# Seven-product pairs in six output projection chunks, row sums of y, rows on three partition groups, and one plan for all attention groups

## The chip, the cores and the metric

The kernel runs on one core of a Trainium2 chip. The metric is the device time of one execution in microseconds (us), taken as the median of the runs. TensorE (PE) multiplies, VectorE (DVE) and ScalarE (ACT) work on the elements, and SyncE (SP) issues most of the DMAs. Everything is in float32; matrix products are made from operands split into a high and a low half (fp32r), three products in place of one.

## The reference

One encoder layer on x of 256 tokens by 4096. The stream is first normalised with an embedding norm; then, cut to what matters:

```python
def hybrid_layer(x, w_in, conv_w, sink, w_out, ln_g, ln_b):
    p = x @ w_in                       # 4096 to 26 chunks of 512
    ...
    y_conv = c_b * centred_short_conv(c_c * c_h, conv_w) * jax.nn.silu(c_z)
    y_attn = banded_window_attention(a_q, a_k, a_v, sink) * jax.nn.silu(a_z)
    y = jnp.concatenate([y_conv, y_attn], axis=-1) @ w_out      # 4096 x 4096
    return layer_norm(DN_ALPHA * x + y, ln_g, ln_b)
```

Two big products, by w_in and by w_out, hold nearly all the work. Between them stand a gated short convolution and a windowed attention with 16 heads in four groups; behind the second stand a residual and a norm.

## The kernel before

**Tiles and steps.** x, normalised and transposed, lies in xT as 32 k-tiles (128 of the 4096 rows of w each), each as high and low halves. The weights stream by in steps. A step of kind "s" is one DMA of 1024 KB (four k-tiles by 512 columns), and 24 matmuls of 512 columns: four k-tiles, two token tiles, three products of halves. A step of kind "S", a pair, is one DMA of 512 KB holding two k-tiles as half blocks, on which VectorE makes four more blocks by sums (lines 133 to 135); seven products of sums then stand in for eight (Strassen's scheme, the two k-tiles and two token tiles by two column halves), 21 matmuls of 256 columns. The scheme needs sums of x's blocks as well (x_sums, line 556, kept in SC) and adds its partial results, collected in the PSUM tile pacc, to the chunk's end (pair_copy on ScalarE, pair_sums on VectorE, lines 592 to 595).

**Stages.** The 26 input chunks come first: K and V with eight "s" steps each, the other 24 in the order "sSsSSsSsSSs", six pairs. While a chunk streams, the attention or convolution work of the chunks before is done between its steps, at step numbers kept in a table (`at`). For an attention group the table is SPREAD, for the last of the four DENSE, which puts the same heads' operations closer together. Then comes the output: seven chunks of 512 columns and two of 256, all "s", 64 steps. y lies where x lay, in xT, in the order Y_ORDER.

**One step of the output loop.** For step j: the matmuls of j (mm_out, lines 809 to 811); functions due at j; SP issues the load of the next step for which a raw weight buffer is free; ScalarE makes the high half of step j + 3 (split_hi, line 149), VectorE its low half (split_lo, line 153). The high and low halves have three buffers each, so the high half of step j + 3 waits for the end of step j. The raw pieces have three buffers (w0, w1, w2) in the output stage, and one or two more in the input stage; a load waits for the low half that was made from its buffer's last piece.

**End of a chunk.** Behind the loop of chunk n, end_out and end_out2 run for both token tiles: residual plus accumulator (line 816), statistics (817), and the product with the norm's gain (821). Then res_load(n + 1) issues five DMAs of 256 KB on SP for the next chunk: three rows broadcast to all partitions (gb) and two pieces of x (xc). residual(n) makes the normalised x from them with three operations a tile (lines 791 to 794), at step 2 of chunk n (step 7 for chunk 0).

**Rows and the tail.** The norm's gain and bias are needed as five rows of halves, which build_rows writes at chunk 1's step 4: a load of 32 × 128 into lnw, a cast and a difference (lines 768 and 769), and small DMAs into `rows` (line 771). The tail (finish_lhs, finish_tr, finish_out) makes a 5-row operand from the statistics, transposes it, and adds its product with rows to R. All four spare PSUM tiles serve it under the name att. The last step's halves are made one step early, into a raw buffer.

What sets the order on each engine is the order of these calls; nothing is rescheduled.

## Time and profile before

| what | us |
|---|---|
| median of 3 runs | 1552.48 (1551.56 to 1552.85) |
| the profiled execution's own time | 1551.65 |
| its span | 1549.9 |
| mean granted clock of TensorE | 0.996 |

A span runs from the first to the last recorded instruction. In the views, a row of the timeline gives start, duration, engine, line, operation, and in brackets the idle time ahead of it with the engine that ended it; a row of waits gives the total, the number and the longest; a group gives busy time, mean in ns, and the idle time before. Of the span, the attention of the last group lies near 500 to 550, the output stage runs from about 1179 on, and the tail from about 1515.

### The profile page before, as it was taken

The page shows a single profiled execution, that of the slowest core. Times are in us where ns is not written, and L with a number is a line of the kernel's source. Part 1 is how long each engine was busy: PE and PEld are TensorE (multiplying, and loading weights), DVE is VectorE, ACT ScalarE, POOL GpSimd, SP SyncE. Part 2 cuts the span into 40 slices and gives each one's busy share as a digit, 9 for nine tenths or more (in the row PEclk, how much of TensorE's full clock was granted, in tenths as well). Part 3 has the DMA queues.
Part 4 walks back from the last instruction along what each step waited for, and adds up shares of the span by engine and source line. Part 5 has one row for each costly group of instructions (what it writes and reads, how often), then busy time and mean ns, then how long its engine had stood idle before and what let it go on. Part 6 is the DMA issues. An engine that isn't in the chain of part 4 may idle for free.

```text
span 1549.9 us, 20599 instructions
## 1 busy us (share of the span) xinstructions
PE 1528.0 (99%) x8478; PEld 1320.0 (85%) x8478; DVE 1223.9 (79%) x1358; ACT 738.6 (48%) x620; POOL 1.3 (0%) x7
## 2 busy tenths in 40 slices
PE   7999999999999999999999999999999999999997
PEld 4888888888888888888888888888888888888896
DVE  8678798888898878898888888888987665566656
ACT  4544546556565555545454445444555333333331
POOL 0000000000000000000000000000000000000000
PEclk9999999999999999999999999999999999999998
DMA  7545554555545456556556565566556565666662
GB/s 300 211 140 194 202 193 177 188 176 184 197 165 189 152 196 239 201 197 224 191 180 214 195 214 199 189 200 214 193 202 260 207 245 220 226 224 226 222 222 109
DMA packets 64078, 312.95 MB, mean 202 GB/s; under 512 B 7696, under 2 KB 11248, under 8 KB 38384
## 3 DMA queue, kind: packets, MB, share of 16 engines
q1 hardware_dynamic: 63408, 310.06, 56.6%
q8 instruction: 66, 1.08, 0.3%
q10 hardware_dynamic: 576, 1.57, 0.3%
q14 instruction: 28, 0.23, 0.0%
HBM read 303.66 MB, written 7.86 MB: 201 GB/s over the span
## 4 chain that ended last, share of the span: by engine, by line
PE 89%; DVE 5%; ACT 2%; issue 2%; DMA 1%; SPq 0%; DVEq 0%; ACTq 0%
PE acc L189 15%; PE acc L191 15%; PE acc L190 14%; PE acc L809 7%; PE acc L811 7%; PE acc L810 7%; PE pacc L214 4%; PE pacc L213 4%; PE pacc L215 4%; PE acc L214 3%; PE acc L213 3%; PE acc L215 3%; DVE wlo L153 2%; ACT whi L149 1%; PE att L420 1%
## 5 line engine op out<-in xcount | busy, mean ns | idle before, releaser
L149 ACT ACTIVATE whi<-w 128x2048 fp32r<-128x2048 f32 (+1 forms) x341 | 623.0, 1827 | 738.0 <-PE acc L191 301.6
L153 DVE TENSOR_TENSOR wlo<-w,whi 128x2048 fp32r<-128x2048 f32 (+1 forms) x341 | 739.6, 2175 | 259.8 <-ACT whi L149 257.9
L189 PE MATMUL acc<-whi,xT 128*128 128x512 f32 x1072 | 424.4, 396 | 0.0
L191 PE MATMUL acc<-whi,xT 128*128 128x512 f32 x1072 | 420.2, 392 | 0.0
L190 PE MATMUL acc<-wlo,xT 128*128 128x512 f32 x1072 | 417.3, 389 | 0.7 <-DVE wlo L153 0.7
L191 PEld LDWEIGHTS acc<-whi,xT 128*128 128x128 f32 x1072 | 201.3, 188 | 46.9
L190 PEld LDWEIGHTS acc<-wlo,xT 128*128 128x128 f32 x1072 | 201.4, 188 | 41.7 <-DVE wlo L153 1.0
L189 PEld LDWEIGHTS acc<-whi,xT 128*128 128x128 f32 x1072 | 201.5, 188 | 37.4
L809 PE MATMUL acc<-whi,xT 128*128 128x512 f32 (+1 forms) x560 | 208.1, 372 | 0.0
L811 PE MATMUL acc<-whi,xT 128*128 128x512 f32 (+1 forms) x560 | 206.9, 369 | 0.0
L810 PE MATMUL acc<-wlo,xT 128*128 128x512 f32 (+1 forms) x560 | 205.3, 367 | 0.4 <-DVE wlo L153 0.4
L810 PEld LDWEIGHTS acc<-wlo,xT 128*128 128x128 f32 x560 | 105.1, 188 | 19.6 <-DVE wlo L153 0.8
L811 PEld LDWEIGHTS acc<-whi,xT 128*128 128x128 f32 x560 | 105.1, 188 | 19.6
L809 PEld LDWEIGHTS acc<-whi,xT 128*128 128x128 f32 x560 | 105.3, 188 | 17.1 <-issue 0.4
L133 DVE TENSOR_TENSOR w<-w 128x512 f32<-128x512 f32 x144 | 98.2, 682 | 0.0
L213 PE MATMUL pacc<-whi,xT 128*128 128x256 f32 x288 | 82.4, 286 | 0.0
L214 PE MATMUL pacc<-wlo,SC 128*128 128x256 f32 x288 | 81.0, 281 | 0.0
L215 PE MATMUL pacc<-whi,SC 128*128 128x256 f32 x288 | 80.8, 280 | 0.0
L213 PE MATMUL pacc<-whi,SC 128*128 128x256 f32 x288 | 80.7, 280 | 0.0
L214 PE MATMUL acc<-wlo,xT 128*128 128x256 f32 x288 | 80.5, 279 | 0.0
L214 PE MATMUL pacc<-wlo,xT 128*128 128x256 f32 x288 | 80.5, 279 | 0.0
L213 PE MATMUL acc<-whi,xT 128*128 128x256 f32 x288 | 80.4, 279 | 0.0
(192 smaller groups left out, 1634.8 us busy)
## 6 DMA issues: line engine op xcount, KB each, us to landing
w<-in_wi SPq DMA_DIRECT2D x134, 1024.0 KB, 4.9
w<-in_ws SPq DMA_DIRECT2D x144, 512.0 KB, 3.3
w<-in_wo SPq DMA_DIRECT2D x64, 1024.0 KB, 4.9
yl<-yd SPq DMA_DIRECT2D x7, 512.0 KB, 6.9
xc<-in_x SPq DMA_DIRECT2D x14, 256.0 KB, 6.5
x<-in_x SPq DMA_DIRECT2D x6, 512.0 KB, 7.3
first<-in_wi SPq DMA_DIRECT2D x2, 1024.0 KB, 8.1
...
```

Source lines behind the costliest of these rows:

```text
L133: nc.vector.tensor_tensor(r[:, 4:6, :], r[:, 1:3, :], r[:, 0:1, :].to_broadcast([P, 2, HW]), op=ALU.add)
L149: nc.scalar.activation(part(j, wh[j]), part(j, raw[j]), AF.Copy)
L153: nc.vector.tensor_tensor(part(j, wl[j]), part(j, raw.pop(j)), part(j, wh[j]).bitcast(F32), op=ALU.subtract)
L189: nc.tensor.matmul(a, xh, hk, start=(first and k == 0), stop=False)
L190: nc.tensor.matmul(a, xh, lk, start=False, stop=False)
L191: nc.tensor.matmul(a, xl, hk, start=False, stop=(last and k == PK - 1))
L213: nc.tensor.matmul(o, ah, hi[:, w, :], start=(opens and p == 0), stop=False)
L214: nc.tensor.matmul(o, ah, lo[:, w, :], start=False, stop=False)
L215: nc.tensor.matmul(o, al, hi[:, w, :], start=False, stop=(closes and last))
L809: nc.tensor.matmul(o, yh, hk, start=(s == 0), stop=False)
L810: nc.tensor.matmul(o, yh, lk, start=False, stop=False)
L811: nc.tensor.matmul(o, yl, hk, start=False, stop=(s == KT - 1))
```

## The change

- In the output, chunks 1 to 6 get four pairs each in place of eight k-tiles: chunk 1 in the order "ssSsSsSsSs", chunks 2 to 6 "sSsSssSsSs". Chunk 0 (eight "s") and the two narrow chunks stay. There are 76 steps instead of 64. A chunk's pairs are gathered by pair_copy and pair_sums as in the input, and plus_res adds the residual to them at the chunk's last step; end_out adds the accumulator.
- The sums of y's blocks are made by x_sums at chunk 0's step 6 and chunk 1's steps 0, 1 and 2 into a new SC of four blocks; scratch is a part of R.
- The high half of step j + 3 is now issued ahead of the functions due at j, and sums(j + 4) ahead of the low half.
- residual takes two operations a tile instead of three, at step 5 of chunk 1 and step 4 of chunks 2 to 6 instead of 2.
- The rows lie on three partition groups (0, 32, 64), so that rows takes 1536 columns instead of 4096; the tail fills three groups of t5. Loading (rows_load, chunk 2 step 4) and splitting (rows_split, chunk 2 step 8) are apart, and 15 small DMAs fill the rows instead of six.
- The tail's PSUM tiles alternate between two pools, and the last chunk's residual tile takes SC's place and is loaded at chunk 7's step 0 instead of chunk 6's step 4. The last step's halves are made in their turn.
- The last attention group uses SPREAD; DENSE goes. open_pc comes three steps later.

```diff
+OUT = 100
+OP = 4
+OUT_ORDERS = ["s" * 8, "ssSsSsSsSs"] + ["sSsSssSsSs"] * 5 + ["", ""]
...
-        bs = [(wpool, f"w{k}") for k in range(N_W)] + (extra if steps[j][0] != "out" else [])
+        bs = [(wpool, f"w{k}") for k in range(N_W)] + (extra if j < N_IN else [])
...
-                (sc(0), 5, p1[:, 1, :], True, False), (x(a, 1), 6, p0[:, 1, :], False, True),
+                (sc(0), 5, p1[:, 1, :], True, False), (x(a, 1) if ci < OUT else sc(3), 6, p0[:, 1, :], False, True),
...
-    DENSE = [(2, q_tr, 0), (3, q_lo, 0), (7, q_tr, 1), (8, q_lo, 1)] + head(0, 4, 5, 6, 7, 8, 9, 10, 12, 13) + head(
-        1, 5, 6, 7, 8, 9, 12, 13, 14, 15) + head(2, 9, 10, 11, 12, 13, 14, 15, 17, 18) + head(
-        3, 11, 12, 13, 14, 15, 16, 17, 19, 20)
...
+        if SC.shape[3] == 4:
+            return halves(SC[:, p, 0, :, :], SC[:, p, 1, :, :], s)
...
-            for t, f, a in SPREAD if g < NG - 1 else DENSE:
+            for t, f, a in SPREAD:
...
-                at(j + 1, open_pc)
+                at(j + 4, open_pc)
...
+    RB = [(0, 0), (0, 1), (0, 2), (32, 0), (32, 1), (32, 2), (64, 0), (64, 1)]
...
-    def build_rows():
-        for src, slots_h, slot_l in ((ln_g, (0, 1), 2), (ln_b, (3,), 4)):
-            w = p2.tile([KT, P], F32, name="lnw")
+    lnw = {}
+
+    def rows_load():
+        for k, src in enumerate((ln_g, ln_b)):
+            w = lnw[k] = R[0:KT, k, D - 4 * P:D - 3 * P]
             nc.sync.dma_start(out=w, in_=src.rearrange("(a b) -> a b", b=P))
-            hl = p2.tile([KT, 2, P], F32R, name="lnhl")
+
+    def rows_split():
+        for k, (slots_h, slot_l) in enumerate((((0, 1), 2), ((3,), 4))):
+            w, hl = lnw[k], R[0:KT, k, D - 3 * P:D - P].bitcast(F32R).rearrange("p (a b) -> p a b", a=2)
             nc.vector.tensor_copy(hl[:, 0, :], w)
             nc.vector.tensor_tensor(hl[:, 1, :], w, hl[:, 0, :].bitcast(F32), op=ALU.subtract)
-            for r in slots_h:
-                nc.sync.dma_start(out=rows[r:r + 1, :].bitcast(F32), in_=hl[:, 0, :].bitcast(F32))
-            nc.sync.dma_start(out=rows[slot_l:slot_l + 1, :].bitcast(F32), in_=hl[:, 1, :].bitcast(F32))
+            for b, a0, n in ((0, 0, 12), (32, 12, 12), (64, 24, 8)):
+                for r, h in [(r, 0) for r in slots_h] + [(slot_l, 1)]:
+                    nc.sync.dma_start(out=rows[b + r:b + r + 1, 0:n * P].bitcast(F32), in_=hl[a0:a0 + n, h, :].bitcast(F32))
...
+            z = p2.tile([P, OP * 2 * 4, HT], F32, name="z", tag="SC").rearrange("p a b -> p (a b)")
...
-            nc.vector.tensor_scalar(xc[:, i, :], xc[:, i, :], musd[:, i, 0:1], musd[:, i, 2:3],
-                                    op0=ALU.subtract, op1=ALU.mult)
-            nc.vector.tensor_tensor(xc[:, i, :], xc[:, i, :], gb[:, 0, :], op=ALU.mult)
-            nc.vector.tensor_tensor(xc[:, i, :], xc[:, i, :], gb[:, 1, :], op=ALU.add)
-
-    oacc = {}
+            nc.vector.scalar_tensor_tensor(xc[:, i, :], xc[:, i, :], musd[:, i, 0:1], gb[:, 0, :],
+                                           op0=ALU.subtract, op1=ALU.mult)
+            nc.vector.scalar_tensor_tensor(xc[:, i, :], xc[:, i, :], musd[:, i, 2:3], gb[:, 1, :],
+                                           op0=ALU.mult, op1=ALU.add)
...
+    def plus_res(n):
+
+        c0, w, _, _ = chunks[n]
+        e = st_.pop(("e", OUT + n))
+        for i in range(2):
+            nc.vector.scalar_tensor_tensor(e[:, i, :], res[n][1][:, i, :], ALPHA, e[:, i, :], op0=ALU.mult, op1=ALU.add)
...
-        nc.vector.scalar_tensor_tensor(r, res[n][1][:, i, :], ALPHA, oacc.pop((n, i)), op0=ALU.mult, op1=ALU.add)
+        a = acc.pop((OUT + n, i))
+        if npairs(OUT + n):
+            nc.vector.tensor_tensor(r, a, r, op=ALU.add)
+        else:
+            nc.vector.scalar_tensor_tensor(r, res[n][1][:, i, :], ALPHA, a, op0=ALU.mult, op1=ALU.add)
...
-        nc.vector.tensor_copy(t5[:, i, 0:3:2], ch.bitcast(F32).to_broadcast([P, 2]))
+        for b in (0, 32, 64):
+            if b:
+                nc.vector.tensor_copy(t5[:, i, b + 1:b + 2], t5[:, i, 1:2])
+            nc.vector.tensor_copy(t5[:, i, b:b + 3:2], ch.bitcast(F32).to_broadcast([P, 2]))
...
-            sh = ps_att.tile([P, 512], F32, name="att")
-            nc.tensor.matmul(sh, lhs5[0:5, i, :], rows[0:5, sl], start=True, stop=True)
+            sh = (ps_att if c % 2 else ps_p).tile([P, 512], F32, name="att" if c % 2 else "pacc")
+            b, k = RB[c]
+            nc.tensor.matmul(sh, lhs5[b:b + 5, i, :], rows[b:b + 5, k * W:(k + 1) * W], start=True, stop=True)
...
+    for k in range(OP):
+        at(N_IN + (6, 8, 9, 10)[k], lambda k: x_sums(k, R[:, 1, D - 4 * S:D]), k)
     for n, (c0, w, pk, j0) in enumerate(chunks):
-        npc = KT // pk
-        for q in range(npc):
-            j = j0 + q
-            mm_out(j, n, (0,) if n == ncs - 1 else (0, 1))
+        us = out_units(n)
+        np_ = sum(u[0] == "opair" for u in us)
+        for t, (kind, _, q) in enumerate(us):
+            j = j0 + t
+            if kind == "opair":
+                mm_pair(j)
+            else:
+                mm_out(j, n, (0,) if n == ncs - 1 else (0, 1))
+            if j + 3 < len(steps):
+                split_hi(j + 3)
             for fn, a in later.pop(j, []):
                 fn(*a)
+            if kind == "opair" and q == np_ - 1:
+                pair_copy(OUT + n)
+                at(j + 1, pair_sums, OUT + n)
+                at(j + 1, plus_res, n)
             if j == N_IN + 5:
                 open_p2()
                 res_load(0)
             loads(j)
-            if j + 3 < len(steps) - 1:
-                split(j + 3)
-            if j + 4 == len(steps) - 1:
-                split(j + 4)
-            if q == (0 if n == ncs - 1 else 7 if n == 0 else min(2, npc - 1)):
+            sums(j + 4)
+            if j + 3 < len(steps):
+                split_lo(j + 3)
+            if t == (0 if n == ncs - 1 else 2 if not np_ and n else (7, 5, 4)[min(n, 2)]):
                 residual(n)
-            if n == 1 and q == 4:
-                build_rows()
+            if n == 2 and t == 4:
+                rows_load()
+            if n == 2 and t == 8:
+                rows_split()
                 nc.scalar.activation(small.tile([P, 1], F32, name="sd", bufs=1), eps_t, AF.Sqrt)
-            if n == ncs - 3 and q == 4:
+            if n == ncs - 2 and t == 0:
                 res_load(ncs - 1)
```

VectorE at the opening of chunk 1. wlo is a low half; R, xc and gb are the output, the residual's x and its rows. Before, from the second end_out of chunk 0 on:

```order
L816 SCALAR_TENSOR_TENSOR R_10252<-xc_10262,acc_10038 128x512
L817 BN_STATS s21_10254<-R_10252 128x6
L821 TENSOR_TENSOR R_10252<-R_10252,gb_10261 128x512
L153 TENSOR_TENSOR wlo_10383<-w0_10268,whi_10381 128x2048
L153 TENSOR_TENSOR wlo_10413<-w1_10298,whi_10411 128x2048
L153 TENSOR_TENSOR wlo_10443<-w2_10328,whi_10441 128x2048
```

Now, from the same place on:

```order
L859 SCALAR_TENSOR_TENSOR R_10249<-xc_10262,acc_10038 128x512
L860 BN_STATS s21_10251<-R_10249 128x6
L864 TENSOR_TENSOR R_10249<-R_10249,gb_10261 128x512
L578 TENSOR_TENSOR R_10249<-xT_86 128x512
L583 TENSOR_TENSOR R_10249<-R_10249 128x128 x4
L446 TENSOR_TENSOR SC_10253<-R_10249,SC_10253 128x512
L154 TENSOR_TENSOR w2_10305<-w2_10305 128x512
L155 TENSOR_TENSOR w2_10305<-w2_10305 128x256
L156 TENSOR_TENSOR w2_10305<-w2_10305 128x256
L174 TENSOR_TENSOR wlo_10399<-w1_10268,whi_10385 128x2048
L578 TENSOR_TENSOR R_10249<-xT_86 128x512
```

The low half of step 3 (wlo_10399, before wlo_10383) stood directly behind end_out; now the x_sums of two k-tiles and the sums of step 4 stand between.

VectorE at the turn from chunk 2 to chunk 3. Before:

```order
L816 SCALAR_TENSOR_TENSOR R_10252<-xc_10625,acc_10635 128x512
L817 BN_STATS s21_10254<-R_10252 128x6
L821 TENSOR_TENSOR R_10252<-R_10252,gb_10624 128x512
L153 TENSOR_TENSOR wlo_10922<-w1_10813,whi_10920 128x2048
L153 TENSOR_TENSOR wlo_10952<-w2_10843,whi_10950 128x2048
L153 TENSOR_TENSOR wlo_10982<-w0_10873,whi_10980 128x2048
```

Now (w0_11090 is the half piece of step 6 of chunk 3, w2_11042 the piece of step 5):

```order
L857 TENSOR_TENSOR R_10249<-acc_10715,R_10249 128x512
L860 BN_STATS s21_10251<-R_10249 128x6
L864 TENSOR_TENSOR R_10249<-R_10249,gb_10704 128x512
L174 TENSOR_TENSOR wlo_11092<-w0_10954,whi_11088 128x1792
L174 TENSOR_TENSOR wlo_11121<-w1_10985,whi_11117 128x2048
L154 TENSOR_TENSOR w0_11090<-w0_11090 128x512
L155 TENSOR_TENSOR w0_11090<-w0_11090 128x256
L156 TENSOR_TENSOR w0_11090<-w0_11090 128x256
L174 TENSOR_TENSOR wlo_11154<-w2_11042,whi_11147 128x2048
```

The sums of step 6 stand ahead of the low half of step 5.

SP at the same turn, before:

```order
L116 DMA w0_10873<-in_wo 128x2048
L781 DMA gb_10885<-in_emb_g_row 128x512
L782 DMA gb_10885<-in_emb_b_row 128x512
L783 DMA gb_10885<-in_ln_g 128x512
L785 DMA xc_10886<-in_x 128x512 x2
L116 DMA w1_10918<-in_wo 128x2048
```

Now:

```order
L137 DMA w2_11042<-in_wo 128x2048
L813 DMA gb_11055<-in_emb_g_row 128x512
L814 DMA gb_11055<-in_emb_b_row 128x512
L815 DMA gb_11055<-in_ln_g 128x512
L817 DMA xc_11056<-in_x 128x512 x2
L135 DMA w0_11090<-in_ws 128x1024
L137 DMA w1_11119<-in_wo 128x2048
```

The five loads of the residual stood ahead of a full piece; now they stand ahead of the half piece on which the sums of step 6 wait.

More of the change, by code (lines that the diff above doesn't have):

```diff
@@ L60, in units, with out_units, npairs @@
     return us
+def out_units(n):
+    if CHUNKS[n] < W:
+        return [("out", OUT + n, q) for q in range(KT * CHUNKS[n] // PIECE)]
+    q, p, us = 2 * npairs(OUT + n) // PK, 0, []
+    for u in OUT_ORDERS[n]:
+        if u == "s":
+            us.append(("out", OUT + n, q))
+            q += 1
+        else:
+            us.append(("opair", OUT + n, p))
+            p += 1
+    assert q == NPC
+    return us
+def npairs(ci):
+    return PAIRS[ci] if ci < OUT else OUT_ORDERS[ci - OUT].count("S")
 IN_STEPS = [u for ci in range(len(IN_ORDER)) for u in units(ci)]
 IN_PIECES = [u[1:] for u in IN_STEPS if u[0] == "in"]
-IN_PAIRS = [u[1:] for u in IN_STEPS if u[0] == "pair"]
 N_IN = len(IN_STEPS)
+OUT_STEPS = [u for n in range(len(CHUNKS)) for u in out_units(n)]
+ALL_PAIRS = [u[1:] for u in IN_STEPS + OUT_STEPS if u[0] in ("pair", "opair")]
+OUT_PIECES = [u[1:] for u in OUT_STEPS if u[0] == "out"]
 @with_exitstack
@@ L83, in encoder_kernel @@
     ctx.enter_context(tc.manual_schedule())
-    steps = list(IN_STEPS)
+    steps = IN_STEPS + OUT_STEPS
     chunks = []
-    c0 = 0
-    for w in CHUNKS:
-        pk = PIECE // w
-        chunks.append((c0, w, pk, len(steps)))
-        for q in range(KT // pk):
-            steps.append(("out", c0 * KT // PIECE, q))
-        c0 += w
+    for n, w in enumerate(CHUNKS):
+        chunks.append((sum(CHUNKS[:n]), w, PIECE // w, steps.index(out_units(n)[0])))
+    is_pair = lambda j: steps[j][0] in ("pair", "opair")
     raw, wh, wl = {}, {}, {}
@@ L112, in load @@
             to = raw[j] = pool.tile([P, PIECE], F32, name=name, bufs=1)
[L113 to L114 removed]
+        if is_pair(j):
+            nc.sync.dma_start(out=to[:, 0:4 * HW], in_=ws[ALL_PAIRS.index((a, b))])
         else:
[L116 removed]
+            nc.sync.dma_start(out=to, in_=wi[IN_PIECES.index((a, b))] if kind == "in" else wo[OUT_PIECES.index((a, b))])
     def loads(j):
@@ L128, in sums @@
     def sums(j):
-        if j >= len(steps) or steps[j][0] != "pair":
+        if j >= len(steps) or not is_pair(j):
             return
@@ L137, in part @@
     def part(j, t):
-        return t[:, HW:] if steps[j][0] == "pair" else t
+        return t[:, HW:] if is_pair(j) else t
     def half_tile(j, name):
@@ L199, in mm_pair @@
         hi, lo = (t.pop(j).rearrange("p (b w) -> p b w", w=HW) for t in (wh, wl))
-        last = p == PAIRS[ci] - 1
+        last = p == npairs(ci) - 1
         if p == 0:
@@ L747, in open_p2 @@
     def open_p2():
-        nonlocal p2, R, st2, ms2, rows, t5, lhs5, ps_att
+        nonlocal p2, R, st2, ms2, rows, t5, lhs5, SC
         ph.close()
         phs.close()
-        pps.close()
-        ps_att = ctx.enter_context(tc.tile_pool(name="ps_att3", bufs=4, space=PSUM))
         p2 = ctx.enter_context(tc.tile_pool(name="p2", bufs=1))
@@ L892, in encoder_kernel @@
     finish_out(1, range(8))
+    pps.close()
 ctx_rows = {}
```

49 lines of the change are left out of this document (29 added, 20 removed).

## The prediction

> **What bounds the kernel now.** I read the busy shares first, then what TensorE waited for, then busy time by stretch.
>
> ```profile
> PE 1528.0 (99%) x8478; PEld 1320.0 (85%) x8478; DVE 1223.9 (79%) x1358; ACT 738.6 (48%) x620; POOL 1.3 (0%) x7
> ...
> PE att L836 <- DVE t L831: 3.2, 1, 3.2
> PE att L516 <- DVE s L482: 1.5, 1, 1.5
> PE att L516 <- ACT p L509: 0.5, 1, 0.5
> PE acc L810 <- DVE wlo L153: 0.4, 1, 0.4
> ```
>
> TensorE is busy 99% of the span, so time is won only with fewer matmul cycles or in the few waits listed. The rest is told by stretches (columns: start:end, stretch, then busy time and count of PE, PEld, DVE, ACT, POOL, the granted clock, DMA share, GB/s):
>
> ```profile
> 515.00:545.00 30.00, 27.87 (x166) 24.27 (x165) 28.52 (x41) 16.67 (x25) 0.00 (x0) 1.00 0.37 123
> 599.50:642.00 42.50, 42.50 (x251) 37.52 (x250) 37.38 (x44) 23.14 (x19) 0.00 (x0) 1.00 0.62 221
> 1240.00:1270.00 30.00, 29.59 (x130) 23.97 (x129) 15.81 (x16) 12.98 (x8) 0.00 (x0) 1.00 0.56 209
> 1284.00:1328.00 44.00, 44.00 (x194) 36.09 (x193) 25.81 (x20) 15.31 (x8) 0.00 (x0) 1.00 0.63 221
> 1537.00:1543.00 6.00, 3.26 (x7) 1.90 (x7) 4.10 (x15) 0.56 (x2) 0.00 (x0) 0.61 0.13 48
> ```
>
> An input chunk with six pairs (second row) keeps VectorE busy 37.4 of 42.5 us, an output chunk without pairs (fourth row) 25.8 of 44. The change takes matmul cycles out of the output and brings VectorE there close to the first figure, while the output stage has three raw weight buffers. So the question is whether VectorE stays ahead.
>
> **Pairs.** Seven products instead of eight:
>
> ```profile
> 612.39 0.28 PE L213 MATMUL pacc<-whi,xT 128*128 128x256 f32 x1
> ...
> 614.87 0.28 PE L213 MATMUL pacc<-whi,xT 128*128 128x256 f32 x1
> ...
> 617.34 0.40 PE L189 MATMUL acc<-whi,xT 128*128 128x512 f32 x1
> ...
> 620.10 0.39 PE L189 MATMUL acc<-whi,xT 128*128 128x512 f32 x1
> ```
>
> A pair takes 614.87 − 612.39 = 2.48 us. Twelve conventional matmuls, which do the same two k-tiles, take 620.10 − 617.34 = 2.76; I take 2.75, a whole "s" step being 5.5 (44 us for eight steps in the fourth stretch). 24 pairs × 0.27 = **−6.5**.
>
> **Last attention group.** The stretch 515 to 545 has 30.00 − 27.87 = 2.1 us without a matmul, of which L516's two waits are 2.0. The spread plan puts those heads' VectorE work further apart: **−2.1**. Ends: 0, if the next steps inherit the work, and −2.1.
>
> **Rows.** The row halves move:
>
> ```profile
> 1260.61 0.21 DVE L768 CAST lnhl<-lnw 32x128 fp32r<-32x128 f32 x1 [5.06 <-DMA lnw<-in_ln_g]
> ...
> 1265.62 0.21 DVE L768 CAST lnhl<-lnw 32x128 fp32r<-32x128 f32 x1 [4.48 <-DMA lnw<-in_ln_b]
> ...
> 1260.85 1.23 SPq L771 DMA_DIRECT2D rows<-lnhl  x2
> ```
>
> VectorE stood 5.06 and 4.48 us there; the third stretch shows that TensorE lost 30.00 − 29.59 = 0.4 by it. Loading four steps earlier removes it: **−0.4**. The 15 small DMAs in place of six cost SP 1.23 / 2 = 0.62 each, 9.3 in all, at the end of chunk 2 (counted below).
>
> **What VectorE gets.** Its durations:
>
> ```profile
> L153 DVE TENSOR_TENSOR wlo<-w,whi 128x1792 fp32r<-128x1792 f32 x144 | 291.1, 2022 | 29.6 <-ACT whi L149 27.7
> L133 DVE TENSOR_TENSOR w<-w 128x512 f32<-128x512 f32 x144 | 98.2, 682 | 0.0
> L135 DVE TENSOR_TENSOR w<-w 128x256 f32<-128x256 f32 x144 | 61.2, 425 | 5.0
> ...
> 1231.82 0.68 DVE L816 SCALAR_TENSOR_TENSOR R<-xc,acc 128x512 f32<-128x512 f32 x1
> ...
> 1235.92 4.49 DVE L153 TENSOR_TENSOR wlo<-w,whi 128x2048 fp32r<-128x2048 f32 x2
> ...
> 530.62 0.41 DVE L592 TENSOR_TENSOR w<-w,pacc 128x256 f32<-128x256 f32 x1
> ...
> 532.32 0.68 DVE L133 TENSOR_TENSOR w<-w 128x512 f32<-128x512 f32 x1
> ...
> 108.62 0.69 DVE L560 TENSOR_TENSOR xs<-xT 128x512 f32<-128x512 f32 x1
> ...
> 110.95 0.56 DVE L425 TENSOR_TENSOR SC<-xs,SC 128x384 fp32r<-128x384 f32 x1 [0.59 <-ACT SC L424]
> ...
> 111.63 2.02 DVE L153 TENSOR_TENSOR wlo<-w,whi 128x1792 fp32r<-128x1792 f32 x1
> ```
>
> So: low half of an "s" step 4.49 / 2 = 2.2, of a pair 1.95 (2.02 less the overlap of neighbours); sums of a pair 0.68 + 2 × 0.42 = 1.5; end_out of both tiles 1235.92 − 1231.82 = 4.1; pair_sums 532.32 − 530.62 = 1.7; x_sums 111.63 − 108.62 = 3.0, its wait for ScalarE's half included; residual, now four operations like L816's, 2.7; plus_res two, 1.25. VectorE runs them in program order, and a low half waits for ScalarE's high half, which waits for a buffer that the step three before leaves:
>
> ```profile
> 1218.35 1.91 ACT L149 ACTIVATE whi<-w 128x2048 fp32r<-128x2048 f32 x1 [3.53 <-PE acc L811]
> ...
> L149 ACT ACTIVATE whi<-w 128x1792 fp32r<-128x1792 f32 x144 | 245.4, 1704 | 256.4 <-PE acc L191 162.4 <-PE pacc L215 41.7 <-DVE w L135 30.3
> ```
>
> A high half takes 1.9, a pair's 1.7, and I put 0.25 between the release and its start.
>
> **Opening of chunk 1.** Zero is its first matmul; its steps s s S s S s begin at 0, 5.5, 11.0, 13.5, 19.0, 21.5. A low half is needed 0.2 after its step begins. Step 1's high half runs from −5.25 to −3.35; behind it on ScalarE stands the half of chunk 0's last x_sums, 0.6, then VectorE's end of it, 0.6, the sums of step 2, 1.5, and low 1, 2.2: it ends at 1.55. From there ends add up (low 2 waits for its high half until 1.95): low 2 3.9, residual 6.6, end_out 10.7, x_sums 13.7, sums of step 4 15.2, low 3 17.4, needed at 13.7: TensorE waits 3.7. TensorE now ends step 3 at 22.7 and step 4 at 25.2. VectorE: x_sums 20.4, low 4 22.4 (in time), x_sums 25.4, sums of step 6 26.9, low 5 29.1, needed at 25.4: 3.7 more. **+7.5**. Before, the same place held end_out and three low halves, 4.1 + 6.6, beside 16.5 us of TensorE, and no wait is listed there. Ends of this term: 0, if the x_sums find gaps that I don't see, and 12, if ScalarE's part comes a high half (1.9) late in two of them.
>
> **Turns into chunks 2 to 6.** At a turn the next chunk's residual rows are loaded, five transfers:
>
> ```profile
> 1276.88 0.33 SPq L781 DMA_DIRECT2D gb<-in_emb_g_row  x1
> ...
> 1278.20 0.90 SPq L785 DMA_DIRECT2D xc<-in_x  x2
> 1279.21 37.81 SPq L116 DMA_DIRECT2D w<-in_wo  x8
> ...
> w<-in_wo SPq DMA_DIRECT2D x1, 1024.0 KB, 8.7
> xc<-in_x SPq DMA_DIRECT2D x2, 256.0 KB, 6.7
> ...
> w<-in_ws SPq DMA_DIRECT2D x144, 512.0 KB, 3.3
> ```
>
> The second xc, issued near 1278.65, lands 6.7 later, at 1285.35: some 8.4 after the first issue of the five. The full piece behind them lands at 1279.21 + 8.7 = 1287.9, 2.5 later; a half piece would take 1.25. Alone, a half piece lands 3.3 after its issue. Before, the piece behind the burst had three steps of lead; now it is the half piece of the pair at step 6, and its sums stand in VectorE's queue ahead of step 5's low half.
>
> Zero is the chunk's first matmul; s S s S s s S begin at 0, 5.5, 8.0, 13.5, 16.0, 21.5, 27.0. With VectorE ahead, low 1 ends as early as ScalarE allows, at −5.5 + 0.25 + 1.7 + 1.95 = −1.6. Then: pair_sums 0.1, plus_res 1.35, sums of 3 2.9, low 2 5.1, end_out 9.2, low 3 11.1, low 4 13.3. The five loads start at 9.2, are in at 17.6, the half piece at 18.9; sums 20.4, low 5 22.6, needed at 21.7: a wait of 0.9, and 1.2 with what chunk 1 leaves. From there VectorE has no lead: low 6 to 9, 0′ and 1′, two sums and the residual are 18.2, plus some 3 for half pieces not yet landed, so low 1′ ends at 0.0 instead of −1.6 and the next wait grows to 2.7. Into chunk 3 the 9.3 us of row DMAs on SP make it 3.5. Sum: 1.2 + 3.5 + 3 × 2.7 = **+12.8**. The first wait moves one for one with the landing. The same additions carried through all steps give a stage 7 shorter for a burst of 7.0 instead of 8.4, 3 longer for 9.0, and 5 less or more for a VectorE 3% quicker or slower.
>
> **Ends.**
>
> ```profile
> 1515.16 2.29 DVE L153 TENSOR_TENSOR w<-w,w 128x2048 fp32r<-128x2048 f32 x1
> ...
> 1539.16 0.16 DVE L831 COPY t<-ch 128x2 f32<-128x2 f32 x1
> ```
>
> The last step's low half ran ahead of chunk 7's end_out; now it stands behind it: **+0.6** (0 to 2.2, one such half). Four more tiny copies like L831's lie before the last transpose, at most 4 × 0.16: **+0.4**. ScalarE's added pair copies lie beside work (48% busy).
>
> **Sum** on the profiled execution (1551.65; its span 1549.9): −6.5 − 2.1 − 0.4 + 7.5 + 12.8 + 0.6 + 0.4 = +12.3, so 1564.0. The median shown is 0.83 higher: **1564.8**.
>
> **Rivals.**
>
> *The clock falls in the new waits (slower still).* The last stretch quoted has a granted clock of 0.61 around L836's 3.2 us wait; that with waits of 1.5 has 1.00. In 6 us at 0.61, 6 × 0.39 = 2.3 us of work are lost. Six waits of 2.7 to 3.7 would lose 14; VectorE catches up meanwhile, so I count half: 1571.5.
>
> The Trainium skill, "TensorE: Matmul & The Clock Gate" (section "HAM oscillation"), has the clock halved after gaps over about 3.4 us and charges half of some 3.4 us, 1.7, each time. By that only the three longest waits would count, an estimate of 3 × 1.7 = 5.1, or 2.6 with half of it caught up: 1567.4. The 3.2 us wait here was followed by 0.61, so the trace does not contradict a limit of about that size, and no run here shows it exactly.
>
> *The burst doesn't hold the half piece (same).* If it lands 3.3 after its issue, as alone, low 5 is ready before 21.7 at each turn and only chunk 1 waits: 1564.8 − 12.8 = 1552.0. Against it: 8.7 for the piece behind the burst, against a median of 4.9 for all such pieces:
>
> ```profile
> w<-in_wo SPq DMA_DIRECT2D x64, 1024.0 KB, 4.9
> ```
>
> *VectorE keeps its lead (faster).* In the second stretch it has 37.4 busy in 42.5 and TensorE never waits. An output chunk now gives it 6 × 2.2 + 4 × 1.95 + 4 × 1.5 + 1.7 + 1.25 + 4.1 + 2.7 = 36.8 in 43. If the halves spread as there, all waits go: 1564.8 − 12.8 − 7.5 = 1544.5. It decides itself at low 5 after a turn: before 21.7 no wait, each later one counts in full. Against it: three buffers, and chunk 1's queue, which does not hang on DMA at all.
>
> **How the numbers follow.** Forecast 0.60 (own range 1557 to 1572: burst, VectorE's pace, the attention term's ends); lower clock 0.13; same 0.14; faster 0.13. 0.2%, about 3 us, is what a measurement of this kernel can tell from no change. To leave out no more than 2 in 10 the range reaches down to the "same" case and up past the clock case: 1552 to 1574. Faster 0.13, same 0.14, slower 0.73.
>
> **What would show it.** Right: waits of conventional L810-type matmuls for the low half at steps 3 and 5 of chunk 1, near 3.7 each, and at step 5 of chunks 2 to 6, 1 to 3.5; VectorE's sums waiting for half pieces there; L516's waits gone; pairs of 2.48. Wrong: an output stage with TensorE busy throughout (VectorE kept its lead), a half piece landing near 3.3 at the turn, a clock under 1.00 inside chunks 1 to 6, or large new waits in the fourth attention group.

## The result and the profile after

| | before | changed |
|---|---|---|
| median, us | 1552.62 (4 runs) | 1570.89 (4 runs, 1570.73 to 1572.62) |
| ratio, 95% interval | | 1.0122 [1.0104, 1.0139] |
| profiled execution, us | 1551.65 | 1571.03 |
| its span, us | 1549.9 | 1569.3 |
| granted clock | 0.996 | 0.991 |

The changed kernel is slower by 18 us, inside the stated range, where 1564.8 was forecast. Its page has:

```profile
PE 1528.5 (97%) x8694; PEld 1328.2 (85%) x8694; DVE 1298.2 (83%) x1494; ACT 759.7 (48%) x642; POOL 1.3 (0%) x7
```

The view of waits, for TensorE and VectorE (total, number, longest):

```profile
PE acc L842 <- DVE wlo L174: 18.8, 7, 5.2
PE att L882 <- DVE t L877: 3.5, 1, 3.5
...
PE acc L842 <- DVE w L174: 0.8, 1, 0.8
...
DVE w L154 <- DMA w<-in_ws: 46.6, 17, 8.8
```

TensorE is idle more, and nearly all of it, 18.8 us, has one reason: seven times an "s" step of the output stood for its low half. VectorE in turn stood 46.6 us for half pieces. L516 is gone from the list. The stretches of the last attention group and of chunks 1 to 6 (columns as in the prediction: stretch, PE, PEld, DVE, ACT, POOL, clock, DMA, GB/s):

```profile
515.00:545.00 30.00, 29.93 (x173) 26.05 (x172) 26.09 (x38) 16.54 (x25) 0.00 (x0) 1.00 0.37 132
1222.45:1273.34 50.89, 45.03 (x229) 38.13 (x228) 45.76 (x58) 20.03 (x14) 0.00 (x0) 0.97 0.51 181
1273.34:1320.24 46.90, 44.71 (x229) 37.99 (x228) 37.30 (x42) 19.97 (x13) 0.00 (x0) 0.96 0.61 210
1320.24:1371.33 51.09, 45.85 (x230) 38.86 (x228) 37.84 (x41) 18.47 (x11) 0.00 (x0) 0.93 0.55 193
1371.33:1416.27 44.94, 43.11 (x229) 36.85 (x228) 35.67 (x36) 18.47 (x11) 0.00 (x0) 1.00 0.61 212
1416.27:1463.47 47.20, 44.73 (x229) 37.99 (x228) 37.83 (x41) 18.48 (x11) 0.00 (x0) 0.96 0.59 210
1463.47:1507.77 44.30, 43.13 (x229) 36.85 (x228) 33.45 (x32) 18.70 (x11) 0.00 (x0) 1.00 0.66 236
```

The chunks should all take 6 × 5.496 + 4 × 2.466 = 42.84 us (a plain chunk of the kernel before took 43.95; both step lengths are from undisturbed steps). What they took beyond is the **loss**, used in the table below: 8.0, 4.1, 8.2, 2.1, 4.4 and 1.5 us, 28.3 in all. A loss holds the wait and the slow matmuls behind it. In four of the six chunks the clock is under 1.00, which the prediction had named as a sign of being wrong.

VectorE in chunk 1, where its opening work piles up, and at the turns into chunks 2, 3 and 4; then SP at the turns into chunks 3 and 4 (start, duration, operation, and the idle time ahead):

```profile
1233.34 0.69 DVE L578 TENSOR_TENSOR R<-xT 128x512 f32<-128x512 f32 x1
1234.07 1.02 DVE L583 TENSOR_TENSOR R<-R 128x128 f32<-128x128 f32 x4
1235.79 0.69 DVE L446 TENSOR_TENSOR SC<-R,SC 128x512 fp32r<-128x512 f32 x1 [0.70 <-ACT SC L445]
1236.39 0.69 DVE L154 TENSOR_TENSOR w<-w 128x512 f32<-128x512 f32 x1
...
1237.92 2.28 DVE L174 TENSOR_TENSOR wlo<-w,whi 128x2048 fp32r<-128x2048 f32 x1
...
1293.45 0.69 DVE L154 TENSOR_TENSOR w<-w 128x512 f32<-128x512 f32 x1 [6.12 <-DMA w<-in_ws]
...
1343.40 0.69 DVE L154 TENSOR_TENSOR w<-w 128x512 f32<-128x512 f32 x1 [8.79 <-DMA w<-in_ws]
...
1344.93 4.22 DVE L174 TENSOR_TENSOR wlo<-w,whi 128x2048 fp32r<-128x2048 f32 x2
...
1391.08 0.69 DVE L154 TENSOR_TENSOR w<-w 128x512 f32<-128x512 f32 x1 [6.29 <-DMA w<-in_ws]
...
1392.61 4.22 DVE L174 TENSOR_TENSOR wlo<-w,whi 128x2048 fp32r<-128x2048 f32 x2
```

```profile
1319.16 11.55 SPq L800 DMA_DIRECT2D rows<-R  x15
1330.82 0.38 SPq L137 DMA_DIRECT2D w<-in_wo  x1
1331.30 0.37 SPq L813 DMA_DIRECT2D gb<-in_emb_g_row  x1
...
1332.89 0.92 SPq L817 DMA_DIRECT2D xc<-in_x  x2
1333.93 0.71 SPq L135 DMA_DIRECT2D w<-in_ws  x1
...
1380.68 0.33 SPq L813 DMA_DIRECT2D gb<-in_emb_g_row  x1
...
1383.01 0.74 SPq L135 DMA_DIRECT2D w<-in_ws  x1
```

In chunk 1 the low half of step 3 begins at 1237.92, when its step has been running since 1235.95: x_sums and sums stand ahead of it, as in the order. At the turns VectorE stands 6.12, 8.79 and 6.29 us at the sums of step 6, and the low half of step 5 comes right behind. In chunk 3 the 15 row DMAs hold SP for 11.6 us first, so that a full piece, the burst and the half piece all start within 3.1 us, and the half piece (issued 1333.93) is there only at 1343.4, 12.1 us after the burst's first load. At the turn into chunk 4, where no row DMAs stand ahead, it is 10.4 (1380.68 to 1391.08); the forecast had 8.4 + 1.25 = 9.65.

### The profile page after: what moved, and what is told of

Same layout as the page of the kernel before. It is cut to its first block, busy times and chain, and to the rows that moved or that the text cites. A ratio compares the mean times of both kernels' runs of the same rounds, so it can differ in the third digit from the quotient of the medians.

```text
span 1569.3 us, 21272 instructions
## 1 busy us (share of the span) xinstructions
PE 1528.5 (97%) x8694; PEld 1328.2 (85%) x8694; DVE 1298.2 (83%) x1494; ACT 759.7 (48%) x642; POOL 1.3 (0%) x7
## 4 chain that ended last, share of the span: by engine, by line
PE 78%; DVE 11%; DMA 5%; ACT 3%; issue 3%; SPq 1%; DVEq 0%; ACTq 0%
PE acc L210 14%; PE acc L212 14%; PE acc L211 14%; DVE wlo L174 5%; PE pacc L235 4%; PE pacc L234 4%; PE pacc L236 4%; PE acc L842 3%; DMA w<-in_ws 3%; PE acc L843 3%; PE acc L841 3%; PE acc L235 3%; PE acc L234 3%; PE acc L236 3%; ACT whi L170 2%
## 5 line engine op out<-in xcount | busy, mean ns | idle before, releaser
L170 ACT ACTIVATE whi<-w 128x2048 fp32r<-128x2048 f32 (+1 forms) x353 | 640.4, 1816 | 730.2 <-PE acc L212 288.8
L174 DVE TENSOR_TENSOR wlo<-w,whi 128x2048 fp32r<-128x2048 f32 (+1 forms) x353 | 759.5, 2161 | 163.3 <-ACT whi L170 161.4
L212 PEld LDWEIGHTS acc<-whi,xT 128*128 128x128 f32 x1072 | 201.3, 188 | 46.8
L211 PEld LDWEIGHTS acc<-wlo,xT 128*128 128x128 f32 x1072 | 201.4, 188 | 41.2 <-DVE wlo L174 1.0
L210 PEld LDWEIGHTS acc<-whi,xT 128*128 128x128 f32 x1072 | 201.5, 188 | 37.9
L842 PE MATMUL acc<-wlo,xT 128*128 128x512 f32 (+1 forms) x464 | 172.5, 372 | 18.8 <-DVE wlo L174 18.8
L843 PE MATMUL acc<-whi,xT 128*128 128x512 f32 (+1 forms) x464 | 172.3, 371 | 0.0
L841 PE MATMUL acc<-whi,xT 128*128 128x512 f32 (+1 forms) x464 | 171.5, 370 | 0.0
L154 DVE TENSOR_TENSOR w<-w 128x512 f32<-128x512 f32 x168 | 114.9, 684 | 46.7 <-DMA w<-in_ws 46.6
L842 PEld LDWEIGHTS acc<-wlo,xT 128*128 128x128 f32 x464 | 88.9, 192 | 36.1 <-DVE wlo L174 21.5
L235 PE MATMUL pacc<-wlo,SC 128*128 128x256 f32 x360 | 101.4, 282 | 0.0
L841 PEld LDWEIGHTS acc<-whi,xT 128*128 128x128 f32 x464 | 89.0, 192 | 14.5 <-issue 0.4
L843 PEld LDWEIGHTS acc<-whi,xT 128*128 128x128 f32 x464 | 89.0, 192 | 14.4
L236 PE MATMUL pacc<-whi,SC 128*128 128x256 f32 x360 | 101.1, 281 | 0.0
L234 PE MATMUL pacc<-whi,SC 128*128 128x256 f32 x360 | 101.1, 281 | 0.0
L234 PE MATMUL acc<-whi,xT 128*128 128x256 f32 x336 | 93.7, 279 | 0.0
L236 PE MATMUL acc<-whi,xT 128*128 128x256 f32 x336 | 93.6, 279 | 0.0
```

The costliest lines, as they stand in the source:

```text
L154: nc.vector.tensor_tensor(r[:, 4:6, :], r[:, 1:3, :], r[:, 0:1, :].to_broadcast([P, 2, HW]), op=ALU.add)
L170: nc.scalar.activation(part(j, wh[j]), part(j, raw[j]), AF.Copy)
L174: nc.vector.tensor_tensor(part(j, wl[j]), part(j, raw.pop(j)), part(j, wh[j]).bitcast(F32), op=ALU.subtract)
L210: nc.tensor.matmul(a, xh, hk, start=(first and k == 0), stop=False)
L211: nc.tensor.matmul(a, xh, lk, start=False, stop=False)
L212: nc.tensor.matmul(a, xl, hk, start=False, stop=(last and k == PK - 1))
```

## The experiments

Each is the changed kernel with the edit shown, but for e7, which starts from the kernel before. Times are medians; the kernel before had 1551.9 to 1552.5 beside them. The loss per chunk is worked out from the traces as above (for plain and other orders with their own step lengths). A trace is of one execution, and some lie away from the median of their run: e1's took 1566.7 us and e2's 1570.2, e6's, the shortest of its four, 1567.5, and f1's, the longest of its eleven, 1557.9.

| run | us | loss in chunks 1, 2, 3, 4, 5, 6 | sum |
|---|---|---|---|
| changed | 1570.9 | 8.0, 4.1, 8.2, 2.1, 4.4, 1.5 | 28.3 |
| e1_chunk1_plain | 1565.1 | 0, 1.1, 9.9, 1.2, 3.6, 6.8 | 22.6 |
| e2_rows_at_3 | 1568.8 | 8.1, 5.2, 4.7, 2.6, 1.6, 4.1 | 26.3 |
| e3_split_in_7 | 1572.6 | 8.0, 3.9, 1.7, 5.2, 1.8, 2.3 | 22.9 |
| e4_filler | 1570.8 | 8.1, 2.2, 6.1, 4.6, 2.8, 3.7 | 27.4 |
| e5_no_burst | 1551.6 | 8.0, 0, 0.8, 0.1, 0.1, 0.1 | 9.0 |
| e6_sums_behind | 1570.8 | 10.3, 2.4, 5.8, 1.9, 2.0, 1.9 | 24.3 |
| e8_plain1_swap | 1556.6 | 0, 0, 4.8, 2.0, 2.6, 3.3 | 12.6 |
| f1_all | 1556.6 | 0, 3.8, 1.7, 0.5, 1.9, 5.4 | 13.4 |
| f2_all_sums_ahead | 1559.0 | 0, 7.1, 2.0, 1.7, 3.9, 2.0 | 16.7 |
| f3_rows_early | 1551.3 | 0, 0, 1.9, 1.7, 1.9, 2.7 | 8.0 |
| f4_two_pairs | 1545.1 | 0, 0, 0, 0, 0, 0 | 0 |
| e7_spread_only | 1549.8 | (no pairs) | |

**e1, chunk 1 plain.**

```diff
-OUT_ORDERS = ["s" * 8, "ssSsSsSsSs"] + ["sSsSssSsSs"] * 5 + ["", ""]
+OUT_ORDERS = ["s" * 8] * 2 + ["sSsSssSsSs"] * 5 + ["", ""]
-        at(N_IN + (6, 8, 9, 10)[k], ...
+        at(N_IN + 9 + k, ...
...
-            if t == (0 if n == ncs - 1 else 2 if not np_ and n else (7, 5, 4)[min(n, 2)]):
+            if t == (0 if n == ncs - 1 else 2 if n > 6 else (7, 5, 4)[min(n, 2)]):
```

The last line keeps chunk 1's residual at step 5.

> Chunk 1 gets eight plain steps again, and the four sums of y stand one each at its steps 1 to 4; the rest is as changed. Theory 1 (VectorE's queue at the opening of chunk 1 is a local debt): the waits at steps 3 and 5 of chunk 1 go, which with the slow step behind the first lost 5.8 + 2.2 = 8.0 us, and four pairs less cost 1.1: about 1564.0 us. Rival (VectorE is short over the whole stage, so the debt turns up at the next turn): the wait in chunk 2 grows by 4 or more and the time stays near 1570.

Measured 1565.11, ratio to before 1.0082 [1.0066, 1.0097], 5.8 less than the changed kernel. Chunk 1 loses nothing now, and chunk 2 loses 1.1 instead of 4.1: the opening's loss doesn't turn up at the next turn, as theory 1 says. Chunks 2 to 6 together lose 2.3 more (22.6 against 20.2) in the traced execution, which is one of the longer two of four (1562.7 to 1566.9); whether a part of the gain of 6.9 is always lost again isn't settled.

**e2, residual loads at step 3.**

```diff
-            if n + 1 < ncs - 1:
+            if n + 1 < ncs - 1 and not npairs(OUT + n + 1):
                 res_load(n + 1)
...
+            if t == 3 and 0 < n < ncs - 1 and np_:
+                res_load(n)
...
-(7, 5, 4)[min(n, 2)]
+7
```

> The five residual loads of chunks 2 to 6 (and of chunk 1) are issued behind the piece loads of the chunk's own step 3 instead of at the turn, and residual comes at step 7. Theory 1 (the half piece of step 6 is late because it stands behind the burst): the waits at step 5 of chunks 2, 4, 5 and 6, which lost 4.05, 2.1, 4.35 and 1.45 us with the slow steps behind them, go, and that of chunk 3 (8.2) falls to what the 15 row DMAs cost, 1 to 4: 1553 to 1556 us. Rival (VectorE has too much work after a turn, whatever lands when): low halves are late all the same, 1562 us or more.

Measured 1568.8, a gain of 2.1 only, where 1553 to 1556 was expected. VectorE's timeline around the turn into chunk 2 tells why:

```profile
1269.99 0.69 DVE L154 TENSOR_TENSOR w<-w 128x512 f32<-128x512 f32 x1 [5.15 <-DMA w<-in_ws]
...
1273.72 0.74 DVE L823 SCALAR_TENSOR_TENSOR xc<-xc,musd,gb 128x512 f32<-128x512 f32 x1
...
1280.33 1.28 DVE L850 SCALAR_TENSOR_TENSOR R<-xc,R 128x512 f32<-128x512 f32 x2
...
1283.05 2.28 DVE L174 TENSOR_TENSOR wlo<-w,whi 128x2048 fp32r<-128x2048 f32 x1
```

The burst now holds up another half piece, that of the next chunk's step 1 (5.15 us), and behind it stand residual, pair_sums and plus_res: the wait moves to step 2. The time is the rival's, but by another mechanism than too much work on VectorE, so this run doesn't decide between the theories; e5 does.

**e3, the row DMAs in chunk 7.**

```diff
+            if n == 7 and t == 1:
+                rows_split()
             if n == 2 and t == 8:
-                rows_split()
```

> rows_split with its 15 small DMAs moves from chunk 2's step 8 to chunk 7's step 1, where SP has few loads left. Theory 1: chunk 3's wait of 5.4 us and the slow step behind it (8.2 in all) fall to what the turns into chunks 2 and 5 lost (4.1 to 4.4), a gain of 4: about 1567 us. Rival (the 15 transfers lie beside the burst and only the burst counts): no change, 1570 to 1571. Second rival (the debt only moves on): chunk 3 gets shorter and chunk 4 longer, gain under 1.5.

Measured 1572.63, where 1567 was expected. Chunk 3's loss falls from 8.2 to 1.7, but chunk 4's rises by 3.1; chunks 2 to 6 together lose 5.4 less. More than that is lost behind: from chunk 7 on, this trace takes 7.6 us longer. The move brought a wait, here in VectorE's timeline and in TensorE's waits and timeline:

```profile
1535.13 0.42 DVE L859 SCALAR_TENSOR_TENSOR R<-xc,acc 128x256 f32<-128x256 f32 x1 [3.20 <-DMA rows<-R]
```

```profile
PE acc L842 <- DVE w L174: 4.4, 1, 4.4
...
1538.73 0.58 PE L842 MATMUL acc<-w,xT 128*128 128x256 f32 x1 [4.42 <-DVE w L174]
1539.11 0.41 PE L843 MATMUL acc<-w,xT 128*128 128x256 f32 x1
1539.32 0.41 PE L841 MATMUL acc<-w,xT 128*128 128x256 f32 x1
```

end_out of chunk 7 writes the part of R from which the row DMAs read, and stands for them; the last step's low half is behind it (4.4 us instead of 0.8). Behind the wait, matmuls start 0.21 us apart instead of 0.12, which costs 2.8 us; with 1.2 for the distance of the narrow chunks' matmuls (last section) this makes up the 7.6, so the slow matmuls are paid in full there. The row DMAs do cost time at the turn; that they aren't hidden is shown, their exact price isn't.

**e4, fillers for the clock.** Matmuls whose results are not read stand ahead of the seven waiting steps.

```diff
+    FILL = {(1, 3): 10, (1, 5): 8, (2, 5): 8, (3, 5): 16, (4, 5): 8, (5, 5): 8, (6, 5): 8}
+            for _ in range(FILL.get((n, t), 0)):
+                f = ps_att.tile([P, W], F32, name="att")
+                nc.tensor.matmul(f, xT[:, 0, 0:P], wh[j][:, 0:W], start=True, stop=True)
```

> TensorE gets 8 to 16 matmuls of 512 columns whose results nobody reads, ahead of the seven steps that waited, so that none of its idle gaps is over 2 us; each filler takes 0.23 us and ends before the low half would come. Theory 1 (VectorE and the landing set the end of each wait; a slow step only gives VectorE the time by which the next wait is shorter): the granted clock in chunks 1 to 6 is 1.00, the waits of chunks 4 and 6 grow by about 1.7, and the time stays within 1.5 us of 1570.9. Rival (slow steps add in full): the 8.2 us that TensorE lost in them are gained, about 1563 us.

Measured 1570.8, as without the fillers and as theory 1 says. Its stretches of chunks 1 to 3:

```profile
1222.71:1273.61 50.90, 48.37 (x247) 40.08 (x246) 45.86 (x58) 20.04 (x14) 0.00 (x0) 1.00 0.56 183
1273.61:1318.61 45.00, 45.00 (x237) 38.35 (x236) 36.53 (x41) 19.97 (x13) 0.00 (x0) 1.00 0.62 216
1318.61:1367.58 48.97, 47.54 (x246) 39.76 (x244) 35.56 (x38) 18.48 (x11) 0.00 (x0) 1.00 0.53 190
```

The clock is 1.00, and chunk 1 still takes 50.9. Chunks 4 and 6, with waits of 2.0 and 1.3 in the changed kernel, lose 2.5 and 2.2 us more than there. In these chunks a slow step and a longer wait are the same time under two names: VectorE and the landing set the end. Fillers were tried on this kernel alone.

**e5, no burst.** The residual loads of chunks 2 to 6 are left out, so the result isn't the layer's.

```diff
-            if n + 1 < ncs - 1:
+            if n < 1 or n == ncs - 3:
                 res_load(n + 1)
+            elif n + 1 < ncs - 1:
+                res[n + 1] = res[n]
```

> Leaves out the residual loads of chunks 2 to 6 (their residual works on chunk 1's rows and x again), so that no five transfers stand at the turns; VectorE's instructions are all there. Theory 1 (a half piece behind the burst is what VectorE stands for at a turn): the waits at step 5 of chunks 2 to 6 go, but for what the row DMAs do in chunk 3: of the 20.2 us lost there 15 to 17 are gained, 1554 to 1556 us. Rival (VectorE's own work after a turn is too much; moving the burst gained 2 us only): waits of 1 to 3 remain at each turn, over 1562 us.

Measured 1551.58, ratio to before 0.9997 [0.9988, 1.0006]: 19.3 us less than the changed kernel, more than expected. Its stretches of chunks 2 and 3:

```profile
1273.26:1316.06 42.80, 42.80 (x229) 36.88 (x228) 37.17 (x42) 20.09 (x13) 0.00 (x0) 1.00 0.58 203
1316.06:1359.65 43.59, 43.15 (x230) 36.87 (x228) 36.80 (x40) 18.60 (x11) 0.00 (x0) 1.00 0.55 190
```

VectorE has all its work (37.17 us in chunk 2, 37.30 in the changed kernel), and yet chunks 2 to 6 lose 1 us together. Nearly the whole loss of the turns needs the burst; the 15 row DMAs, which are still there, cost chunk 3 only 0.8 without it. Whether it is the burst's place ahead of the half piece or its bytes that delay the landing isn't separated.

**e6, sums behind the low half; e8, with e1's edits as well.**

```diff
-            sums(j + 4)
             if j + 3 < len(steps):
                 split_lo(j + 3)
+            sums(j + 4)
```

> In the output loop the sums of step j + 4 stand behind the low half of step j + 3 on VectorE, not ahead of it; nothing else differs. Theory 1 (the low half of step 5 is late because it stands behind sums that wait for a DMA): the waits at step 5 of chunks 2 to 6 go; what is late next is the pair of step 3, whose sums now come behind end_out, by about 1: 1562 to 1566 us. Rival (the landing alone sets the time, wherever VectorE stands for it): no gain, 1570 to 1571.

> Both edits: chunk 1 plain with the sums of y one a step, and sums behind the low half. Theory 1: the gains add, 1565.1 less 5 to 9, so 1555 to 1560, with waits near 1 at step 3 of each chunk and no slow clock. Rival (VectorE is short of time over the stage): the second edit gives nothing on top, 1564 to 1566.

Measured 1570.8 (1567.5 to 1572.5) for e6, where 1562 to 1566 was expected, and 1556.59 for e8, as expected and 8.5 less than e1. In both the waits at step 5 of chunks 2 and 4 to 6 go, and others come at step 3 (most 1.2; none in e8's chunk 2, 3.3 lost with slow matmuls in its chunk 3, where none were expected). In e6 chunk 1 loses 2.3 more. Its traced execution, 3.6 us shorter than the changed kernel's, agrees with its loss, which is 4.0 smaller; the other three took 1570.0 to 1572.5, and no trace shows why. The new order has a price of its own, seen in f1's timeline:

```profile
1342.44 0.42 DVE L156 TENSOR_TENSOR w<-w 128x256 f32<-128x256 f32 x1
1344.77 2.03 DVE L174 TENSOR_TENSOR wlo<-w,whi 128x1792 fp32r<-128x1792 f32 x1 [1.90 <-ACT whi L170]
```

A pair's low half now follows its sums directly on VectorE, and ScalarE's high half needs the sums too, so VectorE stands 1.9 us for ScalarE.

**e7, the spread plan alone**, on the kernel before.

```diff
-            for t, f, a in SPREAD if g < NG - 1 else DENSE:
+            for t, f, a in SPREAD:
-                at(j + 1, open_pc)
+                at(j + 4, open_pc)
```

> The kernel before, with the spread plan for the last attention group and open_pc three steps later, and no other edit. Theory 1: L516's two waits go and nothing comes in their place: 1.5 to 2.1 us less than before, 1550.4 to 1551. Rival (the postponed work makes the convolution stage wait): no difference within 0.5 us.

Measured 1549.8, ratio 0.9986 [0.9977, 0.9995], a gain of 2.1, and no new wait. Its stretch of the last attention group, 27.87 busy before:

```profile
515.00:545.00 30.00, 29.93 (x175) 26.10 (x174) 25.50 (x37) 16.53 (x25) 0.00 (x0) 1.00 0.38 128
```

**f1 to f4, versions meant to be fast.** f1 has e1's and e6's edits, the order "ssSsSsSsSs" in chunks 2 to 6, residual at step 5, the row DMAs in chunk 1 and the last halves a step early. f2 puts the sums ahead again.

```diff
 # f1, beside e1's and e6's edits
-["sSsSssSsSs"] * 5
+["ssSsSsSsSs"] * 5
-(7, 5, 4)[min(n, 2)]
+(7, 5, 5)[min(n, 2)]
...
-            if n == 2 and t == 4:
+            if n == 1 and t == 4:
                 rows_load()
-            if n == 2 and t == 8:
-                rows_split()
+            if n == 1 and t in (6, 7):
+                rows_split(t - 6)
...
+            if j + 4 == len(steps) - 1:
+                split(j + 4)
 # f3, on f1
-(7, 5, 5)[min(n, 2)]
+(7, 5, 7)[min(n, 2)]
-            if n == 1 and t == 4:
+            if n == 0 and t == 6:
                 rows_load()
-            if n == 1 and t in (6, 7):
+            if n == 1 and t in (1, 3):
 # f4, on f3
-["ssSsSsSsSs"] * 5
+["ssssSssSs"] * 5
-    for k in range(OP):
+    for k in range(2):
-(7, 5, 7)[min(n, 2)]
+(7, 5, 5)[min(n, 2)]
```

> Chunk 1 plain with one sum of y a step; chunks 2 to 6 in the order ssSsSsSsSs, so that the first half piece behind the five residual loads is that of step 4 or 6 with a full step more ahead of it; sums behind the low half; residual at step 5; the row DMAs in chunk 1, in two parts; the last step's halves one step early. Theory 1 (only the burst at the turn and the sums standing in front of it cost time): no wait over 1 us is left from chunk 1 to the last chunk; against the kernel before, 5.4 us from 20 pairs and 2.1 from the attention group, less 0.5 to 1.5 for the tail and the rows: 1545 to 1547 us. Rival (VectorE is short of time with four pairs a chunk): waits come back at the end of each chunk, 1551 or more.

> As f1_all, with the sums of step j + 4 ahead of the low half of step j + 3 again. Theory 1 (behind a burst the place of the sums decides): a wait of 1.5 to 3 at step 5 of each of chunks 2 to 6, 6 to 11 us more than f1_all. Rival (with a plain step more ahead the place of the sums is of no matter): within 1 us of f1_all.

> As f1_all, with two edits: residual of chunks 2 to 6 at step 7 instead of 5, where the low half behind it has 6.8 us in hand and not 1 or less, and the row loads in chunk 0, the row splits with their DMAs at chunk 1's steps 1 and 3, away from the first turn. Theory 1 (what is left in f1_all are these two queues): the waits at step 9 of chunks 2 to 6 (1.4 to 2.4 us each) and at the first pair of chunk 2 (1.3) go with the slow steps behind them, about 8 us: 1548 to 1549. Rival (VectorE has no time left with four pairs a chunk, wherever its work stands): the waits come back at other steps, 1553 or more.

> As f3_rows_early, but two pairs in chunks 2 to 6 instead of four, in the order ssssSssSs, with two sums of y and residual at step 5: ten pairs, 2.7 us of TensorE saved, and VectorE gets some 4 us a chunk less. Theory 1 (with a lead of plain steps behind each burst nothing waits): no wait over 1 us in the output stage, and 2.1 from the attention group on top: 1547 to 1548 us. Rival (any half piece costs more than its 0.27 us): 1550 or more, no better than the spread plan alone.

f1 took 1556.6 (1552.0 to 1557.9) and missed: the low half of step 9 is late because residual stands ahead of it, at the place that its rival named (the wait that f3's expectation puts at the first pair of chunk 2 is at step 6, its third). f2 took 1558.95, 2.4 more than f1, between what its theory and its rival said: its sums stand for half pieces again (waits of 1.4 to 4.7 us at step 5), while f1's waits at step 9 are gone. f3 takes 1551.26, ratio 0.9997 [0.9989, 1.0006], between its theory and its rival too: the queues moved help, but with four pairs a chunk waits of about 1 us remain at steps 3 and 7. f4 takes **1545.06**, ratio 0.9954 [0.994, 0.9967], the fastest of all and 2 to 3 less than expected. Its view of waits has no low half in the output stage left; the stretches of chunks 2 and 3:

```profile
1266.29:1309.70 43.41, 43.41 (x211) 36.51 (x210) 30.61 (x28) 18.57 (x12) 0.00 (x0) 1.00 0.62 217
1309.70:1353.08 43.38, 43.38 (x212) 36.47 (x210) 32.52 (x32) 17.09 (x10) 0.00 (x0) 1.00 0.66 225
```

VectorE is busy 32.5 of 43.4 us where it had 37.8 of 51.1 in chunk 3 of the changed kernel. The burst is still there in f4, ahead of a full piece. f4 has fewer pairs and a longer run of plain steps behind the burst; which of the two does more wasn't tried.

## Why the prediction was right in direction and short in size

- **Pairs, −6.5**: right. A pair takes 2.466, two k-tiles 2.748, so 24 × 0.28 = −6.8.
- **Last attention group, −2.1**: right. 29.93 of 30.00 busy in its stretch, and e7 gained 2.1 alone.
- **Rows, −0.4**: right. Chunk 2's first step lost 0.7 in the kernel before and 0.4 in e7, which loads the rows in the same way; in the changed kernel it loses nothing. The small DMAs before were five (two and one for the gain, one and one for the bias, 0.5 to 0.6 us of SP each), not six. The 15 that came instead are in the turns' term.
- **Opening of chunk 1, +7.5**: right in place and size. The two waits are at steps 3 and 5, 4.1 and 2.1 (in the distance of the matmuls' starts), and the slow step behind the first 1.7: 8.0 lost. e4, without slow steps, lost 8.1 there, and e1 took the whole of it away.
- **Turns, +12.8**: the mechanism is right, the size too small; here the forecast failed by 7.4. They lost 20.2 us: 4.1, 8.2, 2.1, 4.4, 1.5 where 1.2, 3.5 and three times 2.7 stood. The five waits alone add up to 13.7, near the forecast, and the other 6.5 are slow matmuls, which the forecast left out. That nearness is luck, since a slow step shortens the next wait: e4, without slow matmuls, lost 2.2, 6.1, 4.6, 2.8 and 3.7, or 19.3. It is luck, too, that the turns into chunks 4 to 6 came out right together (7.9 against 8.1; 11.0 in e4). What was mis-sized is the turn into chunk 3, with the debt that it leaves to chunk 4: of the 6.5 us by which e4 passes the forecast, 4.5 stand there. The 15 row DMAs hold SP 11.6 us, 0.77 each, not 9.3, and they push the piece ahead of the burst into it, so that three loads land together; with the row DMAs elsewhere (e3) the five turns lost 5.4 less. The turn into chunk 2 was short by 2.9: 1.7 are its slow matmuls, and the half piece's sums began 20.1 us into the chunk (1293.45), not at 18.9. e5 shows that the burst is needed for nearly all of it, and VectorE's idle time ahead of the sums that it goes by way of the half piece.
- **Ends, +0.6 and +0.4**: the last step waited 0.8. In the waits the tail's own grew from 3.2 to 3.5; its four copies cost no more than was forecast. Still, from chunk 7 to the end the changed kernel took 61.5 us where it took 61.9 before, among others because the narrow chunks' matmuls stood closer (last section), which gave 1.2 and was in no term.
- **The rival of the clock** saw the event and not its price. The clock did fall, behind the waits of 4.1, 2.35, 5.4 and 2.6 us, and 1571.5 was this rival's number (its own terms, 1564.8 + 14/2, give 1571.8). But with the clock kept at 1.00 (e4) nothing was gained: in this kernel no slow step of chunks 1 to 6 adds to what VectorE and the landing set. That 1570.9 lies near its number is chance. Of e1's four executions the two with a granted clock of 0.994 took 1562.7 and 1563.5 us, the two with 0.991 and 0.992 took 1566.7 and 1566.9; whether slow matmuls lengthen those, or longer waits bring both, isn't shown.
- **The rival of VectorE's lead** asked for half pieces that come in time. e5 shows that it holds in chunks 2 to 6 when they do: without the burst, VectorE kept up with all the pairs' work at four pairs a chunk.
- **The rival of "same"** took the burst to be harmless. e5 says the opposite.

The slow matmuls can be seen directly. Behind the first wait of chunk 1 the starts stand 0.37 and 0.43 apart, where 0.23 is usual:

```profile
1240.26 0.58 PE L842 MATMUL acc<-wlo,xT 128*128 128x512 f32 x1 [3.92 <-DVE wlo L174]
1240.63 0.63 PE L843 MATMUL acc<-whi,xT 128*128 128x512 f32 x1
1241.06 0.63 PE L841 MATMUL acc<-whi,xT 128*128 128x512 f32 x1
```

The Trainium skill, "TensorE: Matmul & The Clock Gate" (section "HAM oscillation"), asks for gaps under some 3.4 us. The price of 1.7 that the prediction gives beside it isn't that section's, which counts 1.67 us of slow time a gap and half of it as lost; it is an estimate, half of the some 3.4 us of sustained work for which the same page's section "What's actually happening" has the clock stay at half speed. That price agrees with three of the four (1.7 each; 2.8 behind the longest). The limit doesn't: waits of 2.35 and 2.6 us brought slow matmuls here, waits of 2.1 and less didn't. Nor is there one limit for all the runs: waits of 2.07 in e8 (chunk 3, step 3) and 2.08 in f2 (chunk 5, step 5) brought them, and one of 3.43 in e1 (chunk 5, step 5; 3.27 of it idle) didn't:

```profile
1432.30 0.51 PE L842 MATMUL acc<-wlo,xT 128*128 128x512 f32 x1 [3.27 <-DVE wlo L174]
1432.65 0.40 PE L843 MATMUL acc<-whi,xT 128*128 128x512 f32 x1
1432.88 0.40 PE L841 MATMUL acc<-whi,xT 128*128 128x512 f32 x1
```
